# A four-layer diffusion step on one core: products by passes, stores from ScalarE, and a recurrence by eights of chunks

## The chip, the cores and the metric

One core of a Trainium2 chip runs the whole step. The metric is device time in microseconds (us) of one execution, the median of a few runs. Engines by their names in the profile: PE is TensorE (PEld its weight loads), DVE VectorE, ACT ScalarE, POOL GpSimd, SP SyncE, which issues most DMAs.

## The reference

Four layers with different mixers act on 128 context and 512 latent tokens (640 columns in all) of width 1024, inner width E = 2048. Each normalises, projects in, mixes, gates with SiLU(z) and projects out:

```python
for i in range(DEPTH):                        # 0 SSD, 1 gMLP, 2 S5, 3 neighbourhood attention
    hc, gate_c = adaln(xc, norm_g[i], cond_ctx @ w_mod[i] + b_mod[i])
    hl, gate_l = adaln(xl, norm_g[i], cond_lat @ w_mod[i] + b_mod[i])
    yc, yl = mixer[i](hc @ w_in[i]), mixer[i](hl @ w_in[i])
    xc = xc + gate_c * (yc @ w_out[i])
    xl = xl + gate_l * (yl @ w_out[i])
```

The third layer (`kind == 2`) is S5: 128 groups of 16 channels, each with 64 complex states, run over time in both directions, then a GLU:

```python
drv = einsum('gnj,blgj->blgn', bb, seq)       # complex drive
drv[:, 0] += ab * h0
s = associative_scan(complex_combine, (ab, drv))   # s[t] = ab * s[t-1] + drv[t]
y = gelu(y_forward + flip(y_backward) + d_skip * uu)
y = y * sigmoid(y @ w_glu + b_glu)
return y * silu(z), final_state
```

The final S5 state of the context is an output too.

## The kernel before

**Units.** All projections go through `stream` (L249). A unit is one weight tile of 128 x 1024, that is 8 blocks of 128 x 128. For fp32 accuracy it is split into `whi` and `wlo`, and the activations into `hhi` and `hlo`; a unit is 8 steps (slots), and a step is three products, (whi, hhi), (whi, hlo), (wlo, hhi), each two matmuls of 320 columns: 48 matmuls a unit. `unit` (L218) makes the parts: SP loads `raw` (two buffers, L212), ScalarE writes `wlo` = -raw, a POOL DMA adds `raw` to it in flight, and ScalarE casts `whi`. Where `N.adds` is off (from the end of layer 3's input stage on) VectorE or POOL subtracts instead. Unit i is made one unit ahead, with three buffers for each part. Units 0 and 1 of a layer, and the last two ahead of a seam, are walked by halves of the columns (`s` not None); `pairs` names three units whose order is changed.

**Layer 3.** `S5.run` (L1610) builds lists of work by slot and `play` (L330) emits them between the slots of the stream. The queues of TensorE, VectorE, ScalarE and POOL keep that order of emission; SP's is ordered by the framework's own planner. PLAN (L1568) is the order of the 32 units of the input projection, u for channels and z for gates: 256 slots. Of each u unit `driven` (L1703) copies the product out, stores it (`ud`) and loads it back as `ur`, turned by chunks of 8 tokens (80 chunks: 64 latent, 16 context). `load_in`, `turn` and `drive` make the drive of a tile of 8 groups into S, [128, 2 directions, 81, 2, 16]. Four u tiles fill one S. When they are there, `scan` (L1732) runs the recurrence over the chunks: 63 steps on VectorE (`steps`, L1752: per direction one product L1758 and two sums L1761), and 16 steps for the context on POOL (`step`, L1763), between the slots that SCAN5 names. Then four responses, OUTS5 giving the slot of each: `load_out` (BC, PQ, Br and `ur` again), `take` (ScalarE and POOL copy S to `zr`), `gen` (POOL and VectorE make `gx`, L1538 and L1551), `answer` (TensorE, L1813), `kernel` (transposes, three copies to `KK`, eight DMAs to `tr`, L1829), `within` (TensorE `t`, L1838; VectorE `r`, L1839; ScalarE's gelu; store to `yd`).

**Turn.** At slot 256 the GLU begins: its first units need y back from `yd`, by `load_y` (L1848, eight DMAs a tile, into the tiles of `hlo` and, for the second four, `gyl`) and `split_y`. `OUT5` and `IN5` are offsets in slots; BG, BM, BY, BI are buffer counts.

Of the kernel before, what the change touches and what calls it, by code (L numbers as in the profile page):

```python
# [117 lines left out]
class Net:  # L118
# [130 lines left out]
    def stream(self, jobs, pairs=None, after=None, ahead=0, cut=None):  # L249
# [46 lines left out]
        for slot in slots:  # L296
            for i, j, s in slot:
# [9 lines left out]
                k = ui * 8 + j  # L307
# [10 lines left out]
                hh, hl = h(k)  # L318
                for wi, (w, hx) in enumerate(((hi, hh), (hi, hl), (lo, hh))):
                    for v, o, c in cols:  # L320
                        mm(p[:m, o:o + c], w[:, j, :], v(hx), start=(k == 0 and wi == 0), stop=(k == 8 * len(units) - 1 and wi == 2))  # L321
# [1261 lines left out]
BG, BM, BY, BI = 3, 4, 2, 3  # L1583


class S5:
# [23 lines left out]
    def run(self, N, h, own, out):  # L1610
# [92 lines left out]
    def driven(self, N, P, p):  # L1703
# [3 lines left out]
        N.nc.sync.dma_start(self.ud[P["kt"]], u)  # L1707
# [24 lines left out]
    def scan(self, N, q, S):  # L1732

        nc, I = N.nc, N.I
# [4 lines left out]
        fin = self.tile(N, [128, 2, 2, 16], "fin", 2)  # L1739
# [12 lines left out]
        def steps(e, c, end, out, tag):  # L1752

            t = [self.tile(N, [128, 2, 32], f"{tag}{d}", 1) for d in range(2)]
            at = c, end - c + 1
            dst = [out[:, d] if out is not None else S[:, d, (c + 1, end - c)[d]] for d in range(2)]
# [6 lines left out]
        def step(e, c, end, out, tag):  # L1763

            src = skew(F[:, :, c, :], 32 * (end - 2 * c + 1))
            dst = out if out is not None else skew(S[:, :, c + 1], 32 * (end - 2 * c - 1))
            t = self.tile(N, [128, 2, 2, 32], tag, 1)
            e.tensor_tensor(t, src[:, None].to_broadcast([128, 2, 2, 32]), A, op=OP.mult)
            for k in range(2):
                e.tensor_tensor(dst, dst, t[:, k].rearrange("p d (r g) -> p d r g", r=2)[:, :, ::1 - 2 * k], op=OP.add)  # L1770
        for c in range(63):
            steps(v, c, 63, None, "sl")
            if c % 4 == 0:
                i = 64 + c // 4
                step(g, i, 143, fin if i == 79 else None, "sc")
                if i == 79:
                    nc.sync.dma_start(N.O["s5"][:, q], fin.rearrange("p d r g -> p d (r g)"))
            yield

    def load_out(self, N, P):  # L1780
        nc, I, kt = N.nc, N.I, P["kt"]
        P["ur"] = self.load_u(N, kt)
# [5 lines left out]
        nc.sync.dma_start(P["B"], N.s5B[:, kt])  # L1788

# [27 lines left out]
    def kernel(self, N, P):  # L1817
# [8 lines left out]
        nc.scalar.copy(KK[:, 112:128], self.D0[:, P["kt"]])  # L1826
        tr = P["tr"] = self.tile(N, [128, 8, 128], "tr", 2)
        for l in range(8):
            nc.sync.dma_start(tr[l::8], KK[:, 16 * (7 - l):16 * (7 - l) + 128])  # L1829

    def within(self, N, P):
# [10 lines left out]
        nc.sync.dma_start(self.yd[kt // 2][kt % 2], ys.rearrange("p g c -> p (g c)"))  # L1842
# [438 lines left out]
```

## Time and profile before

| | us |
|---|---|
| median of 3 runs | 3023.03 (3021.49 to 3030.51) |
| the profiled execution's own time | 3021.86 |
| its span | 3020.1 |
| TensorE busy | 2750.9 (91%), 18412 matmuls |
| VectorE busy | 2051.4 (68%) |
| ScalarE busy | 1472.4 (49%) |
| POOL busy | 1265.0 (42%) |

Layer 1 runs from about 50 to 610 us of the span, its way out to 743, layer 2 to 1180 and its way out to 1320; layer 3's input projection and recurrence to 1884, its GLU to 2085, its way out to 2240; layer 4 to 2885, then the way out and the final norm. A busy share is a mean over all of these. In a group of instructions the idle time is that of the engine just ahead of them, with what ended it; a wait is put down to the releaser that came last. Matmuls overlap, so a mean duration of one is more than their pitch.

### The profile page before, as it was taken

The numbers are of one execution on the slowest core, as the hardware profiler recorded it, in microseconds if no ns is written. First come the engines' busy times: TensorE is split into PE (matmuls) and PEld (weight loads), VectorE is DVE, ScalarE is ACT, GpSimd is POOL, SyncE is SP. The second block draws the span as 40 slices with busy tenths as digits, with TensorE's granted clock in tenths as the row PEclk, the third lists the DMA queues.
The fourth block names the chain that finished last, engine by engine and source line by source line (L and its number), as shares of the span: only waits on it lengthen the run. The fifth ranks groups of instructions, "written<-read, shape, count | busy, mean of one in ns | idle before, by whom it ended". The sixth has DMA issues, their size and how long they took to land. (4 is left out here: it accounts for less than half of the span.)

```text
span 3020.1 us, 50547 instructions
## 1 busy us (share of the span) xinstructions
PE 2750.9 (91%) x18412; PEld 2643.5 (88%) x18412; DVE 2051.4 (68%) x4948; ACT 1472.4 (49%) x2523; POOL 1265.0 (42%) x1452
## 2 busy tenths in 40 slices
PE   6789999999989898999897886999999999999998
PEld 3778888899889888999797776999989999999998
DVE  5987776676689888736877972225956667666842
ACT  5533444444444445356674653444136666666631
POOL 4466666512476773123443540222443333333232
PEclk9899999999999999999898897999999999999999
DMA  7676677687676667968575569323625444444342
GB/s 253 168 186 165 164 182 182 185 283 216 179 214 189 177 195 223 289 194 219 159 215 161 159 162 185 119 92 132 206 85 146 136 130 137 138 129 134 111 179 87
DMA packets 271735, 517.92 MB, mean 171 GB/s; under 512 B 77888, under 2 KB 146944, under 8 KB 270464
## 3 DMA queue, kind: packets, MB, share of 16 engines
q1 hardware_dynamic: 247424, 427.66, 46.2%
q0 software_dynamic: 24064, 87.04, 14.9%
q8 instruction: 146, 2.39, 0.3%
q14 instruction: 101, 0.83, 0.1%
HBM read 333.83 MB, written 65.70 MB: 132 GB/s over the span
## 5 line engine op out<-in xcount | busy, mean ns | idle before, releaser
L321 PE MATMUL acc<-hhi,whi 128*128 128x320 f32 (+2 forms) x3472 | 861.3, 327 | 24.2 <-ACT hhi L204 8.6
L321 PE MATMUL acc<-hhi,wlo 128*128 128x320 f32 (+2 forms) x3472 | 824.2, 317 | 37.7 <-DMA wlo<-raw 36.4
L321 PE MATMUL acc<-hlo,whi 128*128 128x320 f32 (+2 forms) x3472 | 823.8, 317 | 2.5 <-DVE hlo L573 1.3
L321 PEld LDWEIGHTS acc<-hhi,wlo 128*128 128x128 f32 (+1 forms) x3472 | 600.1, 193 | 46.1 <-DMA wlo<-raw 43.5
L321 PEld LDWEIGHTS acc<-hhi,whi 128*128 128x128 f32 (+1 forms) x3472 | 599.0, 195 | 39.9 <-issue 16.5
L321 PEld LDWEIGHTS acc<-hlo,whi 128*128 128x128 f32 (+1 forms) x3472 | 602.9, 194 | 6.8 <-DVE hlo L573 3.1
L205 POOL TENSOR_TENSOR wlo<-raw,whi 128x1024 fp32r<-128x1024 f32 x95 | 244.8, 2578 | 308.9 <-ACT whi L204 295.8
L226 POOL DMA_DIRECT2D wlo<-raw x164 | 145.9, 895 | 540.4 <-ACT wlo L225 497.8
L227 ACT CAST whi<-raw 128x1024 fp32r<-128x1024 f32 (+1 forms) x164 | 170.4, 1039 | 227.5 <-DMA raw<-in_w_mlp_dram 75.4
L225 ACT ACTIVATE wlo<-raw 128x1024 fp32r<-128x1024 f32 (+1 forms) x164 | 173.0, 1056 | 143.0 <-DMA raw<-in_w_mlp_dram 80.9
L433 DVE SCALAR_TENSOR_TENSOR wacc<-wm,conds,wacc 128x512 f32<-128x512 f32 x280 | 222.6, 849 | 19.5 <-DMA wm<-in_w_mod_dram 19.3
L321 PE MATMUL acc<-y,whi 128*128 128x320 f32 (+2 forms) x1024 | 202.3, 314 | 7.0 <-DVE y L205 4.2
L204 ACT CAST whi<-raw 128x1024 fp32r<-128x1024 f32 x125 | 129.4, 1048 | 107.4 <-PE acc L321 84.2
L321 PEld LDWEIGHTS acc<-y,whi 128*128 128x128 f32 x1024 | 163.7, 190 | 9.8 <-DVE y L205 5.1
L1761 DVE TENSOR_TENSOR S<-S,sl 128x32 f32<-128x32 f32 x1008 | 171.3, 224 | 0.0
L909 DVE SCALAR_TENSOR_TENSOR cacc<-pad,vec,cacc 128x644 f32<-128x644 f32 x128 | 154.6, 1208 | 3.8 <-ACT cacc L907 2.0
L2062 ACT ACTIVATE e<-sb,mx 128x384 f32<-128x384 f32 x128 | 78.9, 617 | 96.8 <-DVE mx L2061 94.9
L321 PE MATMUL acc<-y,wlo 128*128 128x320 f32 (+2 forms) x512 | 123.3, 312 | 2.9 <-DMA wlo<-raw 2.8
L1758 DVE TENSOR_TENSOR sl<-S,A 128x64 f32<-128x64 f32 x504 | 125.9, 290 | 0.0
L2095 DVE TENSOR_TENSOR yn<-yn,av 64x128 f32<-64x128 f32 x320 | 90.8, 284 | 42.9 <-ACT yn L2093 34.5
L1876 DVE TENSOR_TENSOR y<-y,sg 128x640 f32<-128x640 f32 x16 | 14.1, 879 | 150.3 <-ACT sg L1875 150.3
L1016 POOL TENSOR_TENSOR dd<-cmat,dt 128x512 f32<-128x512 f32 x80 | 108.4, 1367 | 11.1 <-DVE dt L820 8.6
(407 smaller groups left out, 5504.7 us busy)
## 6 DMA issues: line engine op xcount, KB each, us to landing
wlo<-raw POOLq DMA_DIRECT2D x163, 512.0 KB, 5.3
wm<-in_w_mod_dram SPq DMA_DIRECT2D x96, 512.0 KB, 5.0
raw<-in_w_out_dram SPq DMA_DIRECT2D x64, 512.0 KB, 4.1
raw<-in_w_nat_dram SPq DMA_DIRECT2D x64, 512.0 KB, 3.6
raw<-in_w_ssd_dram SPq DMA_DIRECT2D x48, 512.0 KB, 3.5
raw<-in_w_mlp_dram SPq DMA_DIRECT2D x48, 512.0 KB, 4.0
fb<-fd SPq DMA_DIRECT2D x40, 512.0 KB, 6.3
s5X<-s5gx SPq DMA_DIRECT2D x32, 512.0 KB, 5.5
```

What stands on the lines that cost most here:

```text
L204: (hi_eng or nc.scalar.copy)(hi, src)
L205: (lo_eng or nc.vector).tensor_tensor(lo, src, f(hi), op=OP.subtract)
L225: self.nc.scalar.activation(lo, raw, AF.Copy, scale=-1.0)
L226: self.nc.gpsimd.dma_start(lo, raw, accum_op=OP.add)
L227: self.nc.scalar.copy(hi, raw)
L321: mm(p[:m, o:o + c], w[:, j, :], v(hx), start=(k == 0 and wi == 0), stop=(k == 8 * len(units) - 1 and wi == 2))
L433: e.scalar_tensor_tensor(acc[:, c], w[:, j], a, acc[:, c], op0=OP.mult, op1=OP.add)
L909: nc.vector.scalar_tensor_tensor(acc, pad[:, j:j + 644], w(j), acc, op0=OP.mult, op1=OP.add)
L1016: nc.gpsimd.tensor_tensor(dg.rearrange("p (h l) -> p h l", h=4), N.ident[:, None, :].to_broadcast([128, 4, 128]), self.dt[:, c, 32 * d + 4 ...
L1758: e.tensor_tensor(t[d], F[:, d, at[d], None, :].to_broadcast([128, 2, 32]), A[:, :, d], op=OP.mult)
L1761: e.tensor_tensor(dst[d], dst[d], t[d][:, k].rearrange("p (r g) -> p r g", r=2)[:, ::1 - 2 * k], op=OP.add)
L2095: nc.vector.tensor_tensor(y[r, o], y[r, o], p[r, w:w + 128], op=OP.add)
```

## The change

Four things change.

1. In `stream`, a unit outside the first two, the seam and `pairs` takes its 24 products by passes: (whi, hhi) for all eight blocks, then (whi, hlo), then (wlo, hhi). Each slot still has three products.
2. The stores of `zd`, `ud` and `yd` in layer 3 are issued by ScalarE instead of SP (16 of each).
3. `ur`'s first load is issued two slots after `driven`, its second load six slots after `o` instead of 15 ahead, and the eight DMAs to `tr` three slots after `kernel` (`unroll`).
4. The recurrence goes by blocks of eight chunks: `local` runs seven steps in all ten blocks of a direction at once, `carry` moves the last state of a block to the next block's last, `spread` gives the other seven or eight of a block what came in. It needs the first eight powers of A, which POOL makes beside (`powers`); the context's blocks are in the same instructions, so POOL's 16 steps go. 22 pieces of work are put in 24 places of SCAN5's windows instead of 64. PLAN, OUTS5, SCAN5 and one offset of OUT5 are other numbers; `gx` has 2 buffers for 3, `KK` and `fin` 1 for 2.

```diff
-                hh, hl = h(k)
-                for wi, (w, hx) in enumerate(((hi, hh), (hi, hl), (lo, hh))):
+                items = [(j, wi) for wi in range(3)]
+                if s is None and i >= 2 and not (pairs is not None and pairs <= i < pairs + 3):
+                    items = [((3 * j + x) % 8, (3 * j + x) // 8) for x in range(3)]
+                for kt, wi in items:
+                    k = ui * 8 + kt
+                    hh, hl = h(k)
+                    w, hx = ((hi, hh), (hi, hl), (lo, hh))[wi]
                     for v, o, c in cols:
...
-PLAN = "uuuuuzuuuzzzuuzuuzzuuuuzzzzz"
-OUTS5 = ((80, 8), (139, 7), (188, 8), (228, 7))
-SCAN5 = ((43, 74), (96, 135), (148, 188), (196, 227))
+PLAN = "uuuuuzuuuzzzuuuuzuuuuzzzzzzz"
+OUTS5 = ((78, 8), (122, 7), (176, 8), (218, 7))
+SCAN5 = ((44, 74), (84, 118), (140, 172), (180, 214))
...
-OUT5 = (-15, 0, -5, 0, 5, 7, 9, 17)
+OUT5 = (-15, 0, -2, 0, 5, 7, 9, 17)
...
-BG, BM, BY, BI = 3, 4, 2, 3
+BG, BM, BY, BI = 2, 4, 2, 3
+SX = 1
...
+            put(e + 2, self.load_first, P)
...
-            for i in range(64):
-                put(a + (b - a) * i // 64, lambda N, g: next(g, None), scan)
+            for i in range(24):
+                put(a + (b - a) * i // 24, lambda N, g: next(g, None), scan)
...
+                put_(o + 6, self.load_again, P)
...
+                put_(o + OUT5[6] + 3, self.unroll, P)
...
-        N.nc.sync.dma_start(self.zd[k], z)
+        N.nc.scalar.dma_start(self.zd[k], z)
...
-        N.nc.sync.dma_start(self.ud[P["kt"]], u)
+        N.nc.scalar.dma_start(self.ud[P["kt"]], u)
...
-        fin = self.tile(N, [128, 2, 2, 16], "fin", 2)
+        fin = self.tile(N, [128, 2, 2, 16], "fin", 1)
+        W = self.tile(N, [128, 2, 8, 2, 32], "W8", 1)
...
+        def powers():
+            Wf = W.rearrange("p d b k (r g) -> p d b k r g", r=2)
+            for k in range(2):
+                N.pcopy(Wf[:, :, 0, k, 0], A[:, k, :, 0:16])
+            yield
+            for b in range(1, 8):
+                for d in range(2):
+                    t = self.tile(N, [128, 2, 32], "sc", 1).rearrange("p k (r g) -> p k r g", r=2)
+                    g.tensor_tensor(t, Wf[:, d, b - 1, None, :, 0].to_broadcast([128, 2, 2, 16]),
+                                    A[:, :, d].rearrange("p k (r g) -> p k r g", r=2), op=OP.mult)
+                    g.tensor_tensor(Wf[:, d, b, :, 0], t[:, 0], t[:, 1, ::-1], op=OP.add)
+                if b % 2:
+                    yield
...
+        def move(d, dst, src, w, m):
+            n, nb = m
+            t = self.tile(N, [128, 640], "sx", SX)[:, 0:n * nb * 64]
+            v.tensor_tensor(t.rearrange("p (a b x) -> p a b x", a=n, x=32),
+                            src.rearrange("p a r g -> p a (r g)")[:, :, None, :].to_broadcast([128, n, 2 * nb, 32]),
+                            w.rearrange("p b k x -> p (b k) x")[:, None].to_broadcast([128, n, 2 * nb, 32]), op=OP.mult)
+            t = t.rearrange("p (a b k r g) -> p a b k r g", b=nb, k=2, r=2, g=16)
+            for k in range(2):
+                x, o = (t[:, :, 0, k], dst[:, :, 0]) if nb == 1 else (t[:, 0, :, k], dst[:, 0])
+                v.tensor_tensor(o, o, x[:, :, ::1 - 2 * k], op=OP.add)
+        def local(b):
             for d in range(2):
+                a = 0, -2
+                move(d, places(d, b + 1, a[d], 10)[:, :, None], places(d, b, a[d], 10), A[:, :, d][:, None], (10, 1))
...
+        todo = [lambda b=b: local(b) for b in range(7)]
+        todo += [lambda: carry(1), last]
+        todo += [lambda a=a: carry(a) for a in range(2, 7)]
+        todo += [lambda: spread(9, -1, 7)] + [lambda a=a: spread(a, a, 7) for a in range(1, 7)] + [lambda: spread(7, 7, 8)]
+        beside = powers()
+        for i, f in enumerate(todo):
+            next(beside, None)
+            f()
...
-        KK = self.tile(N, [128, 240], "KK", 2)
+        KK = self.tile(N, [128, 240], "KK", 1)
...
+    def unroll(self, N, P):
         tr = P["tr"] = self.tile(N, [128, 8, 128], "tr", 2)
         for l in range(8):
-            nc.sync.dma_start(tr[l::8], KK[:, 16 * (7 - l):16 * (7 - l) + 128])
+            N.nc.sync.dma_start(tr[l::8], P["KK"][:, 16 * (7 - l):16 * (7 - l) + 128])
...
-        nc.sync.dma_start(self.yd[kt // 2][kt % 2], ys.rearrange("p g c -> p (g c)"))
+        nc.scalar.dma_start(self.yd[kt // 2][kt % 2], ys.rearrange("p g c -> p (g c)"))
```

## Rows read from the trace of the kernel before

**Rows 1.** Stretches: length, busy time (instructions) of five engines, granted clock, DMA share, GB/s.
```profile
743.00:1180.00 437.00, 397.29 (x2628) 388.05 (x2628) 354.38 (x718) 193.54 (x240) 275.29 (x442) 0.95 0.71 198
...
1387.00:1774.00 387.00, 325.51 (x2276) 318.75 (x2275) 339.43 (x1637) 220.88 (x369) 178.23 (x293) 0.90 0.65 176
1774.00:1884.00 110.00, 81.64 (x487) 75.89 (x486) 39.49 (x51) 55.61 (x83) 25.29 (x24) 0.84 0.89 172
```

**Rows 2.** Waits of the whole span: us in total, times, longest.
```profile
PE acc L321 <- DMA wlo<-raw: 43.2, 25, 6.6
```

**Rows 3.** The same view of 743 to 1180 us.
```profile
PE acc L321 <- DMA wlo<-raw: 24.6, 17, 3.6
...
PE D L1449 <- DVE Bb L1516: 9.6, 5, 4.3
```

**Rows 4.** The chain that ended last: start, us, what.
```profile
1863.85 4.28 DMA gyl<-y5d
...
1883.50 194.36 PE acc L321 x1308
```

**Rows 5.** Groups of instructions on the page: busy, mean ns of one, idle before.
```profile
L226 POOL DMA_DIRECT2D wlo<-raw x164 | 145.9, 895 | 540.4 <-ACT wlo L225 497.8
```

**Rows 6.** DMA issues on the page: count, KB each, median us to landing.
```profile
wlo<-raw POOLq DMA_DIRECT2D x163, 512.0 KB, 5.3
```

**Rows 7.** TensorE in order of time: start, us, what, idle before.
```profile
1197.08 0.90 PE L321 MATMUL acc<-yhi,wlo 128*128 128x320 f32 x2 [3.98 <-DMA wlo<-raw]
```

**Rows 8.** VectorE in order of time, in layer 1 and in a scan.
```profile
319.17 3.80 DVE L909 SCALAR_TENSOR_TENSOR cacc<-pad,vec,cacc 128x644 f32<-128x644 f32 x4
...
1708.81 0.19 DVE L1761 TENSOR_TENSOR S<-S,sl 128x32 f32<-128x32 f32 x1
1708.92 0.35 DVE L1758 TENSOR_TENSOR sl<-S,A 128x64 f32<-128x64 f32 x2
1709.19 0.54 DVE L1761 TENSOR_TENSOR S<-S,sl 128x32 f32<-128x32 f32 x4
1709.64 0.35 DVE L1758 TENSOR_TENSOR sl<-S,A 128x64 f32<-128x64 f32 x2
...
1712.54 0.68 DVE L1538 TENSOR_TENSOR gx<-BC,PQ 128x512 f32<-128x512 f32 x1
```

**Rows 9.** Groups of VectorE and POOL between 1387 and 1774 us.
```profile
L1761 DVE TENSOR_TENSOR S<-S,sl 128x32 f32<-128x32 f32 x1008 | 171.3, 224 | 0.0
L1758 DVE TENSOR_TENSOR sl<-S,A 128x64 f32<-128x64 f32 x504 | 125.9, 290 | 0.0
...
L1839 DVE TENSOR_TENSOR r<-yk,t 128x320 f32<-128x320 f32 x22 | 10.1, 482 | 23.3 <-PE t L1838 23.3
...
L1770 POOL TENSOR_TENSOR S<-S,sc 128x64 f32<-128x64 f32 x120 | 42.6, 355 | 9.4
L1768 POOL TENSOR_TENSOR sc<-S,A 128x128 f32<-128x128 f32 x64 | 37.2, 582 | 11.3 <-ACT mT L1701 2.7 <-DVE S L1749 2.2 <-ACT KK L1826 1.7
```

**Rows 10.** VectorE and POOL in order of time, about 1430 us.
```profile
1429.77 4.21 DVE L1758 TENSOR_TENSOR sl<-S,A 128x64 f32<-128x64 f32 x2
...
1430.40 1.36 POOL L1538 TENSOR_TENSOR gy<-BC,PQ 128x512 f32<-128x512 f32 x1
```

**Rows 11.** Waits between 1325 and 1885 us.
```profile
PE t L1838 <- DMA tr<-KK: 20.2, 5, 7.4
```

**Rows 12.** SP's issues in order of time: start, us, what.
```profile
1468.90 5.97 SPq L1829 DMA_DIRECT2D tr<-KK  x8
...
1827.12 3.92 SPq L1853 DMA_DIRECT2D hlo<-y5d  x8
...
1859.37 18.84 SPq L1853 DMA_DIRECT2D gyl<-y5d  x32
```

**Rows 13.** Waits of SP's queue between 1325 and 1885 us.
```profile
SPq L1784 <- DVE gx L1538: 45.6, 6, 15.0
```

**Rows 14.** The instructions of L1707: duration ns min/median/max, first and last start.
```profile
L1707 SPq DMA_DIRECT2D u5d<-r x16: 319/380/572, 1336.3 to 1663.0; - x16
```

More of the change, by code (lines that the diff above doesn't have):

```diff
@@ L306, in stream @@
                     make(x)
-                k = ui * 8 + j
                 base = A0
@@ L317, in stream @@
                     cols = [(cut.ys[s], a, b - a)]
-                hh, hl = h(k)
-                for wi, (w, hx) in enumerate(((hi, hh), (hi, hl), (lo, hh))):
+                items = [(j, wi) for wi in range(3)]
[5 more added lines that the diff above has]
+                    w, hx = ((hi, hh), (hi, hl), (lo, hh))[wi]
                     for v, o, c in cols:
-                        mm(p[:m, o:o + c], w[:, j, :], v(hx), start=(k == 0 and wi == 0), stop=(k == 8 * len(units) - 1 and wi == 2))
+                        mm(p[:m, o:o + c], w[:, kt, :], v(hx), start=(k == 0 and wi == 0), stop=(k == 8 * len(units) - 1 and wi == 2))
+                k = ui * 8 + j
                 step += 1
@@ L1706, in driven, with load_first @@
         N.nc.scalar.copy(u, p)
-        N.nc.sync.dma_start(self.ud[P["kt"]], u)
+        N.nc.scalar.dma_start(self.ud[P["kt"]], u)
+    def load_first(self, N, P):
         P["ur"] = self.load_u(N, P["kt"])
@@ L1750, in scan @@
         yield
[L1752 to L1756, printed above, removed]
-            for d in range(2):
-                e.tensor_tensor(t[d], F[:, d, at[d], None, :].to_broadcast([128, 2, 32]), A[:, :, d], op=OP.mult)
-            for k in range(2):
-                for d in range(2):
-                    e.tensor_tensor(dst[d], dst[d], t[d][:, k].rearrange("p (r g) -> p r g", r=2)[:, ::1 - 2 * k], op=OP.add)
@@ L1763, in step @@
[L1763 to L1777, printed above, removed]
+        def powers():
[11 more added lines that the diff above has]
+                    yield
+            Wf = W.rearrange("p d b k (r g) -> p (d b) k r g", r=2)
+            N.pcopy(Wf[:, :, 0, 1], Wf[:, :, 0, 0])
+            g.tensor_scalar(Wf[:, :, 1, 1], Wf[:, :, 1, 0], -1.0, 0.0, op0=OP.mult, op1=OP.add)
+            yield
@@ new lines, in places @@
+        def places(d, b, a0, n):
+            if d == 0:
+                return S[:, 0, 8 * a0 + b:8 * (a0 + n - 1) + b + 1:8]
+            return S[:, 1, 64 - 8 * (a0 + n - 1) - b:64 - 8 * a0 - b + 1:8]
+        def move(d, dst, src, w, m):
[8 more added lines that the diff above has]
+                v.tensor_tensor(o, o, x[:, :, ::1 - 2 * k], op=OP.add)
@@ new lines, in local, with carry @@
+        def local(b):
+            for d in range(2):
+                a = 0, -2
+                move(d, places(d, b + 1, a[d], 10)[:, :, None], places(d, b, a[d], 10), A[:, :, d][:, None], (10, 1))
+        def carry(a):
+            for d in range(2):
+                if a > 1:
+                    o, i = places(d, 7, a, 1), places(d, 7, a - 1, 1)
+                elif d == 0:
+                    o, i = S[:, 0, 15:80:64], S[:, 0, 7:72:64]
+                else:
+                    o, i = S[:, 1, 49:66:16], S[:, 1, 57:74:16]
+                move(d, o[:, :, None], i, W[:, d, 7:8], (2 if a == 1 else 1, 1))
@@ new lines, in spread, with last @@
+        def spread(af, ab, nb):
+            for d, a in enumerate((af, ab)):
+                o = S[:, 0, 8 * a:8 * a + 8] if d == 0 else S[:, 1, 57 - 8 * a:65 - 8 * a][:, ::-1]
+                move(d, o[:, None, 0:nb], places(d, 7, a - 1, 1), W[:, d, 0:nb], (1, nb))
+        def last():
+            t = self.tile(N, [128, 640], "sx", SX)[:, 0:128].rearrange("p (k d x) -> p k d x", k=2, d=2)
+            v.tensor_tensor(t, skew(F[:, :, 79, :], 32 * -14)[:, None].to_broadcast([128, 2, 2, 32]), A, op=OP.mult)
+            for k in range(2):
+                v.tensor_tensor(fin, fin, t[:, k].rearrange("p d (r g) -> p d r g", r=2)[:, :, ::1 - 2 * k], op=OP.add)
@@ new lines, in scan @@
+        todo = [lambda b=b: local(b) for b in range(7)]
[6 more added lines that the diff above has]
+            f()
+            if i == 15:
+                nc.sync.dma_start(N.O["s5"][:, q], fin.rearrange("p d r g -> p d (r g)"))
@@ L1781, in load_out @@
         nc, I, kt = N.nc, N.I, P["kt"]
-        P["ur"] = self.load_u(N, kt)
         P["U"] = self.tile(N, [128, 2, 2, 8, 16], "BC", 2)
@@ L1788, in load_out, with load_again @@
         nc.sync.dma_start(P["B"], N.s5B[:, kt])
+    def load_again(self, N, P):
+        P["ur"] = self.load_u(N, P["kt"])
     def take(self, N, P):
@@ L1826 @@
         nc.scalar.copy(KK[:, 112:128], self.D0[:, P["kt"]])
+        P["KK"] = KK
+    def unroll(self, N, P):
         tr = P["tr"] = self.tile(N, [128, 8, 128], "tr", 2)
         for l in range(8):
-            nc.sync.dma_start(tr[l::8], KK[:, 16 * (7 - l):16 * (7 - l) + 128])
+            N.nc.sync.dma_start(tr[l::8], P["KK"][:, 16 * (7 - l):16 * (7 - l) + 128])
     def within(self, N, P):
```

## The prediction

> **What bounds the kernel now.** Read the stretches first [rows 1]. In layer 2 (743 to 1180 us) TensorE is busy 397 of 437 us at a granted clock of 0.95; in layer 3's input stage (1387 to 1774) only 325 of 387 at 0.90, and in its turn to the GLU (1774 to 1884) 82 of 110 at 0.84. In that input stage VectorE has most: 339 of 387. So time can come from TensorE's short waits ahead of layer 3, and from layer 3. The GLU behind it runs one matmul each 0.149 us without a wait (194.36 us for 1308) [rows 4]; nothing is to be had there.
>
> Then the waits. TensorE waits 43.2 us, 25 times, longest 6.6, for `wlo` [rows 2], 24.6 us of it in layer 2 [rows 3]. In layer 3 the chain runs through VectorE's recurrence (L1758, L1761) to 1774, then through SP's small transfers.
>
> **Products by passes.** No matmul, load or byte is added: a unit's 24 products are reordered so that `wlo` is first read by the 17th, 32 matmuls later, 32 x 0.149 = 4.8 us. `wlo` is late rather than `whi` because behind ScalarE's first pass it needs POOL's issue, 0.90 us, and 5.3 us of landing [rows 5, 6]; `whi` needs only ScalarE's second pass. So a wait under 4.8 us ends locally. Some 10 of the 43 us lie where the old order stays (a layer's seam, the units of `pairs`: 3.98 us at 1197 is one [rows 7]) or in layer 3, counted below; 33 can go. What is late next: the raw tiles (two buffers) and, in layer 2, VectorE's tables, for which TensorE already waits 9.6 us in five places [rows 3] and which an earlier TensorE meets sooner. The bounds are 0 (all given back to VectorE) and 33 plus some 5 for a clock that dips less. I take somewhat more than half: **-18 us**.
>
> **The recurrence.** Before, a scan is 63 steps of two products (64 elements a partition) and four sums (32), the two directions alternating. From one step to the next 0.72 us pass [rows 8], 63 x 0.72 = 45.4 us. The rows also show the hop: a sum that needs a product starts 0.27 us after it, while of two independent products the second follows at 0.13 (0.35 for both, 0.22 each). Four dependent 644-element operations take 3.80 us, a pitch near 0.95 [rows 8].
>
> After, 129 instructions: 7 `local` x 2 directions of one product of 640 and two sums of 320; 16 `spread` of 448 (two of them 512) and twice 224; 10 `carry` of 64 and twice 32; two of 128 and twice 64, and `last`. Each needs the one before it, and one buffer (`sx`) serves both directions. Durations lie on a line between 0.19 (32 elements) and 0.68 (512) [rows 8]: 640 gives 0.81, 448 0.61, 320 0.48, 224 0.39, 128 0.29, 64 0.22. With 0.05 us more a hop: 14 x 1.92 = 26.9, 16 x 1.54 = 24.6, 10 x 0.75 = 7.5, 1.8 and 0.9: 61.7 us. If a product need not wait for the sums ahead of it (0.13 less, 43 times) 56; if no hop showed at all (129 x 0.13) 45. I take 58, since the rows show the hop: 12.5 us more a scan, **+50 for four**. There are fewer instructions, but twice the elements.
>
> POOL's part shrinks. Its 64 steps took 37.2 + 42.6 us [rows 9]; the new powers are 32 short instructions a scan, by the same rows some 0.25 to 0.35 us each, 12 us a scan, 48 in all. POOL and VectorE get in each other's way: while POOL made three products of 512 (1.36 us each), one pair of VectorE's took 4.21 us in place of 0.35 [rows 10]. So 32 us less POOL is worth 0 to 32; short operations leave gaps, and I take 0.4 of it: **-13**. The collisions with POOL's response products stay.
>
> **The plan and SP.** VectorE then has 339 + 37 = 376 us of work in a stretch that took 387 with 48 idle. Of that idle time 23.3 us is `r` waiting for TensorE's `t` [rows 9], which itself waits 20.2 us for `tr` [rows 11], whose eight issues cost SP 5.97 us a time [rows 12]; and SP stood 45.6 us, 15.0 at the longest, behind `BC`'s buffer [rows 13], with the raw tiles behind it. The change takes 48 stores off SP at 0.38 us each [rows 14], 18 us, with their waits, issues `ur`'s load later, and leaves fewer empty slots (the four scans fill 130 of 170 slots, before 141 of 184). I take 16 us of idle time to remain: **-32**. The ends are 48 (nothing won) and 5.
>
> What the moves add: ScalarE issues 48 stores. No row shows ScalarE issuing; the nearest is SP's 0.32 to 0.57 us [rows 14], so 0 to 27 us on an engine that is busy 221 of 387; I take nothing on the path, but behind each issue `zr`, `mT` and the next unit's casts queue. `KK` has one buffer for two: the next `KK` copy waits until eight issues (5.97) are through and landed, and all that is behind it on ScalarE waits too. The kernels are 7 or 8 slots of 387/184 = 2.1 us apart, some 15 us, and `unroll` is issued 3 slots later: 0 to 3 us of slack, so 0 to 40 us in 16 times, 0 taken. `gx` with two buffers for three makes POOL wait for TensorE's `answer`, with `wlo`'s issue behind it; the passes are the cover, 4.8 us.
>
> **The turn.** Before, 109 us pass from the last step (1774) to the steady GLU (1883.5), through `tr` and 64 small loads of y; the last 32 alone hold SP 18.84 us [rows 12]. After, the last `within` stands at slot 256 in place of 266, but 42 slots remain behind the scan in place of 29. A slot without waits is 325 x 0.90 / 184 = 1.6 us; 37 slots to 251, where the first y tile is free, 59; then 2, four times 3.92 for the first loads [rows 12], 18.8 for the others, 4.3 of landing [rows 4] and 1.5 for a split (two operations of 640): 101 us. **-8**, between -25 (loads issued ahead) and +5.
>
> **Sum.** Layer 3: 50 - 13 - 32 - 8 = -3, and about -1 for its own `wlo` waits. With the passes' -18: -22 against the profiled execution's 3021.86 us (span 3020.1; the median of the runs is 3023.03): **3000 us**.
>
> **Rivals.** *Slower: the long hop.* The recurrence becomes the stage's clock. If a scan takes 62 us (+65 in all) and 40 us of idle time stay, layer 3 changes by 65 - 13 - 8 - 5 = +39; with -16 by passes about 3045. It decides at 58 us a scan with 35 idle: above both, layer 3 eats the passes. For it: 339 of 387 busy, and the hop. Against: 48 us idle, much of it behind SP.
>
> *Nothing net.* The waits only move: `wlo`'s becomes one for tables or raw tiles, and layer 3 pays for its scan what its plan gains: 3016, from 3012 to 3028.
>
> *Shorter: the cost per instruction decides.* As a mechanism of this kernel: if each VectorE instruction held its engine for its whole duration, a step would cost 2 x 0.22 + 4 x 0.19 = 1.20 us, 76 a scan, and the new one 129 durations, 55 us: 21 less in place of 12 more, 84 in four, of which some 35 reach the end before TensorE and SP take over; with 18 by passes and 18 by plan and turn about 2951. Against it stands the pitch of 0.72; for it, that the scans' groups are busy 171.3 and 125.9 us now, collisions included [rows 9]. [...]
>
> **How the numbers follow.** The forecast (2980 to 3014) 0.45, shorter 0.17, nothing net 0.18, slower 0.20. Half of "shorter" lies below 2950 and half of "slower" above 3042: the range is 2950 to 3042. Measurement of this kernel tells about 0.3%, 9 us, from no change. Faster is 0.42 of the forecast's, 0.17 and 0.02: 0.61; the same 0.19; slower 0.20.
>
> **What would show it.** Passes: TensorE's waits for `wlo` below 12 us, those for VectorE's tables above 10. Recurrence: about 58 us of VectorE a scan without collisions, a pitch near duration plus 0.05; POOL's own part near 12. Plan: `r` waiting for `t` below 15 us, the last scan's end about 1760 (1740 to 1785), the steady GLU some 101 us later. The prediction falls if `KK` copies stand first among ScalarE's waits, if `wlo`'s issue waits on POOL behind `gx`, or if sums follow products without a gap.

## The result, and the profile after

The changed kernel takes 3078.26 us (median of 4, 3073.97 to 3081.86) where the kernel before took 3024.99 beside it: ratio 1.0161, interval 1.0142 to 1.0179, 53 us slower where 22 faster was forecast. Its profiled execution took 3077.96 us (span 3075.9). In the code behind the edits line numbers have moved: L321 is now L326, L1538 and L1551 are L1544 and L1557, L1758 and L1761 are L1797 and L1803, L1829 is L1900, L1839 is L1910, L1853 is L1924.

The same three stretches as in [rows 1]: layer 2, the recurrences (from the first to the end of the last), and the way from there to the GLU.

```profile
743.00:1180.00 437.00, 392.53 (x2597) 384.57 (x2598) 351.37 (x718) 188.43 (x233) 273.56 (x441) 0.95 0.70 195
...
1395.00:1806.00 411.00, 318.38 (x2185) 311.55 (x2183) 339.88 (x640) 217.71 (x363) 168.81 (x217) 0.87 0.57 160
1806.00:1936.00 130.00, 94.53 (x566) 89.40 (x567) 47.70 (x56) 61.71 (x91) 31.95 (x29) 0.80 0.78 173
```

Layer 2 is not shorter: from its first `ln_s` to its last `mixl` it takes 425.0 us for 420.6. The recurrences' stretch takes 411 us for 387, with VectorE busy as long as before (340) and idle 71 for 48; the way to the GLU takes 130 for 110. TensorE waits more in both: its busy share falls from 84 to 77% and from 74 to 73%, and the mean granted clock with it (0.90 to 0.87, 0.84 to 0.80).

TensorE's waits of layer 2 (743 to 1184 us), as [rows 3]:

```profile
PE D L1455 <- DVE Bb L1522: 17.5, 8, 4.5
...
PE acc L326 <- DMA wlo<-raw: 4.8, 4, 2.5
```

The waits for `wlo` went from 24.6 to 4.8 us there; those for VectorE's table rose from 9.6 to 17.5. Over the whole span, as [rows 2], the 43.2 us became:

```profile
PE acc L326 <- DMA wlo<-raw: 7.4, 7, 2.5
```

VectorE in the first recurrence, in order of time, as [rows 8]:

```profile
1397.30 0.82 DVE L1797 TENSOR_TENSOR sx<-S,A 128x640 f32<-128x640 f32 x1
...
1399.21 0.82 DVE L1797 TENSOR_TENSOR sx<-S,A 128x640 f32<-128x640 f32 x1
```

A `local` move repeats after 1.91 us; the sum worked with 1.92. The whole of VectorE's instructions of the four recurrences (`sl` before, `sx` after, with the sums into S; busy time behind the length of the stretch):

```profile
1387.00:1774.00 387.00, 258.64 (x1512) 0.90 0.65 176
...
1395.00:1806.00 411.00, 260.95 (x516) 0.87 0.57 160
```

So before, a scan took VectorE 64.7 us in its place, not the 45.4 of undisturbed steps. Beside POOL's steps for the context a step took 1.11 us (1386.83 to 1387.94) where an undisturbed one takes 0.72 [rows 8]:

```profile
1386.83 0.32 DVE L1758 TENSOR_TENSOR sl<-S,A 128x64 f32<-128x64 f32 x2
...
1387.05 0.53 POOL L1768 TENSOR_TENSOR sc<-S,A 128x128 f32<-128x128 f32 x1 [2.71 <-ACT mT L1701]
...
1387.94 0.51 DVE L1758 TENSOR_TENSOR sl<-S,A 128x64 f32<-128x64 f32 x2
```

The first scan, 45.4 us if nothing disturbed it, ran from 1386.8 to 1446.9: 60.1 us. After the change the first one takes 64.8 (1395.2 to 1460.1).

Groups of VectorE and POOL from 1395 to 1806, as [rows 9]:

```profile
L1803 DVE TENSOR_TENSOR S<-S,sx 128x320 f32<-128x320 f32 (+3 forms) x336 | 146.9, 437 | 11.5
...
L1544 DVE TENSOR_TENSOR gx<-BC,PQ 128x512 f32<-128x512 f32 x36 | 33.3, 952 | 24.0 <-PE y L1881 24.0
...
L1910 DVE TENSOR_TENSOR r<-yk,t 128x320 f32<-128x320 f32 x22 | 10.0, 482 | 19.2 <-PE t L1909 16.5 <-issue 2.6
...
L1776 POOL TENSOR_TENSOR sc<-W,A 128x64 f32<-128x64 f32 x53 | 33.8, 639 | 3.5
L1778 POOL TENSOR_TENSOR W<-sc 128x32 f32<-128x32 f32 x54 | 26.0, 482 | 4.2
```

`r` waits less for `t` (16.5 for 23.3), but `gx` now waits 24.0 us for TensorE. Before, with three buffers, it was 3.1:

```profile
L1538 DVE TENSOR_TENSOR gx<-BC,PQ 128x512 f32<-128x512 f32 x38 | 31.2, 846 | 3.2 <-PE y L1813 3.1
```

Of VectorE's 71 idle us, 54 are such waits (47.5 before); the other 17 are gaps of some 0.03 us ahead of each of the recurrence's 516 instructions (11.5 us ahead of the sums), which the old steps do not have (0.0 in [rows 9]). With these gaps a new scan takes 69.5 us in its place. POOL's powers take 0.64 and 0.48 us an instruction, not the 0.25 to 0.35 assumed.

SP's issues on the way to the GLU, as [rows 12], and the end of the chain:

```profile
1862.44 6.55 SPq L1900 DMA_DIRECT2D tr<-KK  x8
1871.92 2.18 SPq L1900 DMA_DIRECT2D tr<-KK  x3
1874.98 5.62 SPq L1924 DMA_DIRECT2D hlo<-y5d  x8
1880.64 3.10 SPq L1900 DMA_DIRECT2D tr<-KK  x5
1883.85 17.63 SPq L1924 DMA_DIRECT2D hlo<-y5d  x24
1902.01 22.42 SPq L1924 DMA_DIRECT2D gyl<-y5d  x32
```

```profile
1925.23 4.53 DMA raw<-in_w_glu_dram
...
1929.84 1.05 ACT whi L204
...
1932.93 12.21 PE acc L326 x73
```

The first 8 of the 64 loads of y stand among the issues of the last `tr`, the other 56 in one line behind it, and behind them the weight tile of the GLU with which the chain goes on. Before, the first 32 were issued by 1836, beside the last responses.

### The profile page after: what moved, and what is told of

Same layout as the page of the kernel before. It is cut to its first block, busy times and chain, and to the rows that moved or that the text cites. A ratio compares the mean times of both kernels' runs of the same rounds, so it can differ in the third digit from the quotient of the medians.

```text
span 3075.9 us, 49413 instructions
## 1 busy us (share of the span) xinstructions
PE 2757.1 (90%) x18412; PEld 2646.2 (86%) x18412; DVE 2096.3 (68%) x3952; ACT 1478.3 (48%) x2525; POOL 1271.4 (41%) x1388
## 4 chain that ended last, share of the span: by engine, by line
PE 32%; DVE 29%; DMA 10%; POOL 8%; ACT 7%; issue 6%; SPq 1%; ACTq 0%; DVEq 0%; POOLq 0%
PE acc L326 25%; DVE S L1803 4%; DVE sx L1797 3%; DVE wacc L439 3%; DMA wlo<-raw 2%; DVE e L2135 2%; DMA wm<-in_w_mod_dram 2%; POOL dd L1022 2%; DVE cacc L915 2%; POOL dd L1029 1%; ACT e L2133 1%; DVE sb L2130 1%; DVE yn L2166 1%; DVE pt L205 1%; ACT zr L1615 1%
## 5 line engine op out<-in xcount | busy, mean ns | idle before, releaser
L326 PE MATMUL acc<-hhi,whi 128*128 128x320 f32 (+2 forms) x3472 | 630.3, 322 | 26.7 <-DVE x L610 9.8
L326 PE MATMUL acc<-hlo,whi 128*128 128x320 f32 (+2 forms) x3472 | 635.7, 320 | 2.5 <-DVE hlo L579 1.7
L326 PE MATMUL acc<-hhi,wlo 128*128 128x320 f32 (+2 forms) x3472 | 609.2, 316 | 7.2 <-DMA wlo<-raw 7.2
L326 PEld LDWEIGHTS acc<-hhi,whi 128*128 128x128 f32 (+1 forms) x3472 | 547.9, 195 | 37.3 <-issue 14.2
L326 PEld LDWEIGHTS acc<-hlo,whi 128*128 128x128 f32 (+1 forms) x3472 | 547.6, 194 | 9.2 <-DVE hlo L579 4.0
L326 PEld LDWEIGHTS acc<-hhi,wlo 128*128 128x128 f32 (+1 forms) x3472 | 540.1, 192 | 13.8 <-DMA wlo<-raw 9.0
L326 PE MATMUL acc<-y,whi 128*128 128x320 f32 (+2 forms) x1024 | 177.9, 314 | 7.2 <-DVE y L746 3.1
L326 PEld LDWEIGHTS acc<-y,whi 128*128 128x128 f32 x1024 | 157.9, 191 | 10.3 <-DVE y L746 4.5
L2135 DVE TENSOR_SCALAR e<-e,mx 128x384 f32<-128x384 f32 (+1 forms) x160 | 154.3, 964 | 4.2
L1803 DVE TENSOR_TENSOR S<-S,sx 128x320 f32<-128x320 f32 (+3 forms) x336 | 146.9, 437 | 11.5
L1881 PE MATMUL y<-zr,gx 128*128 128x112 f32 x512 | 75.0, 305 | 60.4 <-ACT S L1615 18.5
L1881 PEld LDWEIGHTS y<-zr,gx 128*128 128x128 f32 x512 | 70.6, 217 | 64.5 <-issue 19.5
L1547 POOL TENSOR_TENSOR s5gy<-Bu,Qt 128x512 f32<-128x512 f32 x64 | 88.5, 1415 | 58.9 <-DVE s5gx L1557 58.0
```

Of the source, the lines that this page charges most:

```text
L326: mm(p[:m, o:o + c], w[:, kt, :], v(hx), start=(k == 0 and wi == 0), stop=(k == 8 * len(units) - 1 and wi == 2))
L1803: v.tensor_tensor(o, o, x[:, :, ::1 - 2 * k], op=OP.add)
L1881: nc.tensor.matmul(p[:, 112 * g:112 * g + 112], x[:, d, g], zr[:, d, 4 * s + g], start=(d == 0), stop=(d == 1))
L2135: nc.vector.tensor_scalar(e[:, :w], e[:, :w], m[:, 3:4], None, op0=OP.mult)
```

## The experiments

The ratios go by runs of the kernel before made beside each (their medians lie from 3024.99 to 3029.86). Two lengths are read in each trace: layer 3 from its first copied product (the first `r` of `driven`) to the first `sg` of the GLU, and from the last sum `r` of `within` to that `sg`. They come from rows like these, of the changed kernel (duration ns min/median/max, first and last start):

```profile
L1716 ACT COPY r<-acc x16: 677/696/711, 1340.1 to 1687.4; 128x640 f32<-128x640 f32 x16
...
L1946 ACT ACTIVATE sg<-acc,vec x16: 795/797/797, 1939.5 to 2145.1; 128x640 f32<-128x640 f32 x16
...
L1910 DVE TENSOR_TENSOR r<-yk,t x32: 474/484/489, 1515.8 to 1894.3; 128x320 f32<-128x320 f32 x32
```

| kernel | us, median | ratio to before, interval | layer 3 to the GLU | last r to sg |
|---|---|---|---|---|
| before | 3024.99 | 1 | 551.8 | 29.8 |
| e1 passes alone | 3023.43 | 0.9986 (0.9970 to 1.0003) | 548.4 | 29.8 |
| e10 later loads alone | 3028.18 | 1.0005 (0.9990 to 1.0020) | 551.7 | 30.2 |
| e15 stores alone | 3037.60 | 1.0037 (1.0023 to 1.0051) | 560.8 | 29.5 |
| e18 store of u alone | 3031.21 | 1.0004 (0.9990 to 1.0019) | 557.7 | 30.1 |
| e19 stores of z and y alone | 3031.07 | 1.0015 (1.0003 to 1.0028) | 554.5 | 29.6 |
| e2 stores and later loads | 3038.25 | 1.0030 (1.0013 to 1.0046) | 562.5 | 28.7 |
| e3 recurrence and buffers alone | 3057.70 | 1.0099 (1.0074 to 1.0124) | 576.6 | 34.0 |
| e16 the same, interleaved | 3047.69 | 1.0065 (1.0049 to 1.0082) | 569.3 | 34.4 |
| changed, old recurrence (e5) | 3057.22 | 1.0097 (1.0072 to 1.0122) | 584.1 | 44.2 |
| changed, old recurrence and buffers (e9) | 3054.00 | 1.0091 (1.0066 to 1.0116) | 577.0 | 46.3 |
| changed, old plan (e8) | 3063.16 | 1.0109 (1.0077 to 1.0140) | 588.6 | 34.4 |
| changed, last responses later (e14) | 3072.64 | 1.0144 (1.0129 to 1.0160) | 594.1 | 29.8 |
| changed, stores on SP (e20) | 3077.29 | 1.0163 (1.0141 to 1.0186) | 602.7 | 42.9 |
| changed | 3078.26 | 1.0161 (1.0142 to 1.0179) | 599.4 | 45.2 |
| e12 passes up to the turn | 3015.46 | 0.9961 (0.9946 to 0.9977) | 548.6 | 28.6 |

Where no two lines differ in code, single executions still scatter: the first `r` of the eight profiled kernels without passes, whose code ahead of it is the same, starts from 1335.6 to 1349.2 us (mean 1343.6), and the profile of before is the earliest of them. With passes it is 1329.5 to 1342.5 in eight, mean 1336.3. So the 4.5 us that the changed kernel seems to be late there says nothing; on average the passes gain 7. They do so ahead of layer 2, whose first `ln_s` starts at 755.5 us on average with passes and 763.8 without; layer 2 itself takes 427.1 us with them and 425.0 without.

**Passes alone (e1).**

```diff
+                items = [(j, wi) for wi in range(3)]
+                if s is None and i >= 2 and not (pairs is not None and pairs <= i < pairs + 3):
+                    items = [((3 * j + x) % 8, (3 * j + x) // 8) for x in range(3)]
```

> The kernel before with the products by passes and nothing else. My prediction's term is -18 us (bounds 0 to -38). The trace of the whole change puts the first driven 4.5 us LATER than before although TensorE's waits for wlo shrank from 43 to 7 us. Theory 'waits move' (the time goes to other waits of TensorE, whi and VectorE's tables above all, and layer 4's VectorE work gets slower): 3020 to 3033, no gain. Theory 'passes gain, and something else in the change loses it': 3000 to 3010, and the first driven before 1325 us.

3023.43 us, 4 us faster (9 faster to 1 slower). Layer 3 is 3.4 us shorter and what lies ahead of it some 7, but from the first `sg` to the end it takes 1140.3 us for 1132.7: 7.6 are given back (some 5 by all traces: 1137.3 on average in the seven with passes there, 1132.0 in the nine without). In layer 4 (2240 to 2890 us) VectorE's scaling of `e` is slow:

```profile
L2070 DVE TENSOR_SCALAR e<-e,mx 128x384 f32<-128x384 f32 (+1 forms) x160 | 152.3, 952 | 4.2
```

In order of time, one of them and POOL beside it:

```profile
2500.72 2.57 DVE L2070 TENSOR_SCALAR e<-e,mx 128x384 f32<-128x384 f32 x1
...
2500.67 2.40 POOL L205 TENSOR_TENSOR wlo<-raw,whi 128x1024 fp32r<-128x1024 f32 x1 [0.76 <-ACT e L2068]
```

There `wlo` comes from a subtraction on POOL. With passes this one starts behind ScalarE's `e` and so beside VectorE's, which takes 2.57 us; in the trace of before, with POOL idle, the same scaling takes 0.40 and 0.42 us (at 2502.30 and 2505.33). Of the time that POOL waits ahead of these subtractions in layer 4, `e` ends 60.3 of 113.1 us in the changed kernel; before, `whi` ended 162.1 of 174.8. Without passes the group's mean is 625 ns (before, and e12 below). The first theory, that the waits move, has it in the main; the 7 us ahead of layer 3 are a real gain.

**Passes up to the turn, and a second queue (e12).**

```diff
-                if s is None and i >= 2 and not (pairs
+                if s is None and self.adds and i >= 2 and not (pairs
...
-            N.nc.sync.dma_start(f(lo[16 * i:16 * i + 16])
+            (N.nc.scalar if k >= 4 and i % 2 else N.nc.sync).dma_start(f(lo[16 * i:16 * i + 16])
```

> The kernel before with products by passes only while POOL's transfer makes wlo (up to the turn to the GLU), and with half of the last 32 small loads of y issued by ScalarE beside SyncE. Passes everywhere gained 9 us up to the last sg and gave 7 back in layer 4, where VectorE's e (952 ns in place of 625) runs against POOL's subtraction. Theory 'they collide': the give-back goes, and the turn loses up to 9 of its 18.8 us of loads: 3003 to 3015 where before takes about 3028, ratio about 0.994. Rival 'the gain ahead of layer 3 is a wait that comes back anyway, and the landing, not the issue, ends the turn': 3020 to 3026.

3015.46 us, 0.9961 (0.9946 to 0.9977): 12 us faster, and the best kernel here. The give-back is gone (1131.9 us from `sg` to the end), and so is its cause:

```profile
L2070 DVE TENSOR_SCALAR e<-e,mx 128x384 f32<-128x384 f32 (+1 forms) x160 | 99.9, 625 | 4.3
```

The second queue brought nothing that shows: layer 3 is as long as in e1 (548.6 and 548.4), so the 12 us are those of the passes. SP's issue of all 32 in e1, then the two queues with 16 each in e12:

```profile
1849.81 18.94 SPq L1859 DMA_DIRECT2D gyl<-y5d  x32
```

```profile
1857.85 17.86 SPq L1859 DMA_DIRECT2D gyl<-y5d  x16
...
1856.74 17.09 ACTq L1859 DMA_DIRECT2D gyl<-y5d  x16
```

Half the loads held SP 17.86 us, all of them 18.94. So the number of loads that SP issues is not the price that I read from [rows 12]; what paces them is not shown.

**Queues: stores and later loads (e2), later loads alone (e10), stores alone (e15), and their parts (e18, e19).** The edits are the `scalar.dma_start` lines and `load_first`, `load_again`, `unroll` of the change; e18 moves the store of `ud` only, e19 those of `zd` and `yd`.

> The kernel before with the three kinds of stores issued by ScalarE and the dependent loads later (ur two slots after driven and six after o, the eight DMAs to tr three slots after kernel); scan, plan and buffers as before. Theory 'the scan is the clock': the queues are not the cause, 3010 to 3030. Rival 'ScalarE pays for the stores' (48 issues at up to 0.57 us, with zr, mT and casts behind them): 3035 to 3055.

> The kernel before with only the later loads (ur two slots after driven and six after o, the eight DMAs to tr three slots after kernel); the stores stay on SyncE. Together with ScalarE's stores this cost 10 us, and TensorE waited 38 us for tr where it waited 20. Theory 'tr comes too late': the later loads alone cost it, 3033 to 3045, and the wait for tr stays above 35. Rival 'ScalarE pays for the stores': 3022 to 3030, the wait for tr back near 20.

> The kernel before with only the three stores issued by ScalarE; loads where they were. Later loads alone cost nothing, stores and later loads together 10 us, of which some 7 arise between the second and the third copied unit: there SyncE issued two loads of ix and the responses' tables ahead of the first ur, and TensorE waited for it. Theory 'ScalarE's stores alone do it' (an issue takes 0.33 us of ScalarE's queue, and SyncE's order changes with them): 3035 to 3042. Rival 'only both together do': 3024 to 3032.

> The kernel before with one store of three, that of u (ud), issued by ScalarE; those of z and y stay on SyncE, loads where they were. All three together cost 10 us. Behind ud stands a load of the same data (ur), on SyncE; behind zd and yd stand loads some 100 us later or at the turn. Theory 'SyncE issues the dependent load later once the store is not its own' (the third copied unit 24 us behind the first, where before it was 19): ud alone costs most of it, 3034 to 3042. Rival 'every issue on ScalarE costs its 0.33 us and what stands behind it': a third of the 10, 3028 to 3033, the third unit near 19 to 20.

> The kernel before with the stores of z and y issued by ScalarE and that of u on SyncE. All three cost 10 us, u alone 1 (-3 to +6). Theory 'the stores of z and y cost the rest' (at the turn SyncE's loads of y follow a store that is no longer its own): 3034 to 3040, the third unit at 19 us again, the time from the last r to the first sg or the last units longer. Rival 'they only cost together, SyncE's order being another with all three gone': 3025 to 3032.

The later loads cost nothing, although TensorE's wait for `tr` rises to 37.5 us (20.2 in [rows 11]): that wait costs no time here, against the theory of e10. The stores alone cost some 10 us (7 to 15), as expected. Their issue is cheap, 0.33 us each on ScalarE; but the load that depends on them goes out later. In order of time, e10, where SP issues the store:

```profile
1349.88 0.32 SPq L1710 DMA_DIRECT2D u5d<-r  x1
...
1353.26 0.37 SPq L1684 DMA_DIRECT2D ur<-u5d  x1
```

and e2, where ScalarE does (`ur` 5.4 us behind the store for 3.4):

```profile
1344.67 0.35 ACTq L1710 DMA_DIRECT2D u5d<-r  x1
...
1350.05 0.37 SPq L1684 DMA_DIRECT2D ur<-u5d  x1
...
1357.22 3.67 PE L1730 MATMUL drv<-ur,mT 128*128 128x80 f32 x16 [3.66 <-DMA ur<-u5d]
```

It is not the order of SP's queue alone that does it: this store landed 5.3 us behind its issue (3.3 in e10), and SP stood waiting for that (its waits from 1343 to 1352 us):

```profile
SPq L1684 <- DMA u5d<-r: 3.9, 2, 3.5
```

The third unit is copied 26 us behind the first (e2, e18), 24 (e15), but 19 in before, e10 and e19. So the store of u does this, as expected. In e18's trace layer 3 keeps 5.9 us of these 7 (557.7 for 551.8), while its median is 1 us above before (3 less to 6 more). e19 costs 4.5 us (1 to 8.5), 2.7 by its layer 3. By the medians the two parts are some 6 of the 10, by layer 3 8.6 of 9.0: a cost that arises only with all stores moved is not shown.

**The recurrence alone (e3), and interleaved (e16).** e3 takes `scan` with its 24 places, `gx` in 2 buffers and `KK` in 1 into the kernel before. In e16 the directions alternate:

```diff
-            for d in range(2):
-                move(d, ...)
+            both(*[(d, ...) for d in range(2)])      # two products, then sums of k=0 for both, of k=1 for both
-            t = self.tile(N, [128, 640], "sx", SX)
+            t, at, made = self.tile(N, [128, 896], "sx", SX), 0, []
```

> The kernel before with the new recurrence in its old windows, and the buffers that make room for it (gx 2 for 3, KK 1 for 2); plan and queues as before. Theory 'the scan is the clock': a scan has 61.7 us of dependent VectorE work in place of 45.4, so the last scan ends 30 to 60 us later than 1774 and the time is 3055 to 3080. Rival 'the plan and the turn cost it': 3020 to 3040, since the windows are those of before.

> The kernel before with the new recurrence and its smaller buffers, as in the run that took 3058, but with the two directions interleaved: both products, then the four sums in turn, so that no sum directly follows what it needs. For room the products are kept in 896 elements (local goes by 7 and by 3 blocks: twice the instructions there) and A, h0 and fin share fewer buffers. Theory 'the hop': by the durations in the trace, with 0.09 us less for each instruction that need not wait, a scan takes some 48 us of VectorE in place of 61.7, and of the 30 us that the recurrence cost at least half comes back: 3028 to 3044. Rival 'elements, GpSimd's powers or the smaller buffers cost it, not the hop': a scan still takes 58 or more, the time 3050 to 3060.

In e16 the final state of one direction starts from the state's row instead of the last drive, so that this output differs; the instructions are as many. e3 costs 30 us, e16 20. Two `spread` moves in e3, and in e16 the same two directions:

```profile
1433.57 0.62 DVE L1786 TENSOR_TENSOR sx<-S,W 128x448 f32<-128x448 f32 x1
1434.23 0.82 DVE L1792 TENSOR_TENSOR S<-S,sx 128x224 f32<-128x224 f32 x2
1435.09 0.63 DVE L1786 TENSOR_TENSOR sx<-S,W 128x448 f32<-128x448 f32 x1
...
1436.60 0.63 DVE L1786 TENSOR_TENSOR sx<-S,W 128x448 f32<-128x448 f32 x1
...
1440.28 4.26 DVE L1792 TENSOR_TENSOR S<-S,sx 128x224 f32<-128x224 f32 x2
```

```profile
1431.45 1.16 DVE L1788 TENSOR_TENSOR sx<-S,W 128x448 f32<-128x448 f32 x2
1432.52 1.29 DVE L1795 TENSOR_TENSOR S<-S,sx 128x224 f32<-128x224 f32 x4
1433.85 1.16 DVE L1788 TENSOR_TENSOR sx<-S,W 128x448 f32<-128x448 f32 x2
```

The six instructions repeat after 2.40 us interleaved and 3.03 in a chain (1433.57 to 1436.60): the hop is 0.63 / 6 = 0.10 us an instruction. The first recurrence runs from 1396.64 to 1461.43 in e3, 64.8 us, of which one meeting with POOL's products is 3.4: 61.4. In e16 it is 58.4, less 3.5 for the same: 54.9, not the 48 expected, since the 7 + 3 blocks double `local`'s instructions and ran 3.74 us for 3.83. So a third of the 30 us is the hop's. The other 20 are not VectorE's time in the recurrence: in e16 that is 249 us for the four scans, less than the 259 of before. Its waits are longer (65 us for 47.5), most of all the one of `gx` for TensorE:

```profile
1396.70:1800.00 403.30, 249.36 (x684) 0.89 0.63 169
...
L1538 DVE TENSOR_TENSOR gx<-BC,PQ 128x512 f32<-128x512 f32 x38 | 38.5, 1039 | 23.2 <-PE y L1878 23.2
```

Two buffers of `gx` for three, and pieces of work that are longer and stand between fewer slots, both go with it; these two runs do not part them. In e3 the scans take 272.7 us with their gaps, 14 more than before: the theory's 45.4 us for the old scan holds for undisturbed steps only.

**The change with the old recurrence (e5), and with its buffers too (e9).**

> The changed kernel with the recurrence of before (63 steps on VectorE, 16 on POOL, in 64 places of the new windows); passes, queues, plan and the smaller buffers stay. Theory 'the scan is the clock': the last scan's end comes back from 1806 towards 1775, the time is 3020 to 3045. Rival 'plan, turn and buffers cost it': 3060 to 3080, with the last scan ending near 1800 and the turn still above 125 us.

> The changed kernel with the recurrence of before, and with gx in 3 and KK in 2 buffers again; passes, queues and plan stay. With the smaller buffers it took 3057. Theory 'the smaller buffers cost' (in that run VectorE and POOL waited 58 us for TensorE ahead of gx, none of it before the change): 3035 to 3047, those waits gone. Rival 'plan and turn cost': 3052 to 3060, the waits only move.

With 63 steps again 21 us come back, and 32 us of layer 3's loss stay: both theories had a part. The buffers bring 3 us of the whole (within the noise; 7 in layer 3), the rival's way. These waits are in e5; in e9 VectorE's is 5.1 us and POOL's is gone:

```profile
DVE gx L1544 <- PE y L1827: 37.4, 9, 8.7
...
POOL gx L1544 <- PE y L1827: 20.8, 5, 7.8
```

58 us of waits on two engines, 3 us of time: most of them moved.

**The change with the old plan (e8), with its last responses later (e14), with its stores on SP (e20).**

```diff
-OUTS5 = ((78, 8), (122, 7), (176, 8), (218, 7))
+OUTS5 = ((78, 8), (122, 7), (176, 8), (228, 7))
```

(This is e14; e8 puts PLAN, OUTS5, SCAN5 and OUT5 back, e20 the three `sync.dma_start`.)

> The changed kernel with the numbers of before for PLAN, OUTS5, SCAN5 and OUT5; passes, queues, new recurrence and the smaller buffers stay. So far: passes alone -5, queues alone +10, recurrence with its smaller buffers in the old windows +30, the whole change +53; the change with the old recurrence still +29. Theory 'the plan exposes the turn' (the stream reaches slot 251, and the first loads of y, only behind the last responses; those 64 loads then stand bare on SyncE): the plan costs some 15 to 25 us of the whole, so 3052 to 3064, the time from the last r to the first sg falls from 45 to about 30. Rival 'the parts only add, the plan helps the new recurrence for which it was laid out': 3075 or more.

> The changed kernel with one number changed: the last four responses begin at slot 228 in place of 218, as before the change, so that the input projection (TensorE's slots up to 251, which free the tiles of the first y) ends ahead of the last responses and the first 32 loads of y run beside them. Theory 'the plan exposes the turn': the time from the last r to the first sg falls from 45 to about 30 us and 10 to 16 us come back: 3062 to 3068. Rival 'the responses are the stage's end and simply come 10 slots later': the last r is up to 20 us later and the time 3075 to 3095.

> The changed kernel with its three stores back on SyncE; passes, later loads, recurrence, buffers and plan stay. Theory 'the parts add': 10 us come back, 3064 to 3071. Rival 'in the new plan SyncE is the tighter queue, which the stores relieve there': 3076 or more.

The old plan gives 15 us back. In layer 3 it is 11, all between last `r` and `sg` (45.2 to 34.4): the last `r` comes 554.2 us behind the first copy with either plan. e14, by one number, brings that way to 29.8, as expected, but the last `r` comes 10 us later (564.3 us), so 5.6 of 15 remain (their intervals overlap): theory and rival each to about a half. SP in e14:

```profile
1861.15 17.34 SPq L1924 DMA_DIRECT2D hlo<-y5d  x24
1883.24 6.22 SPq L1900 DMA_DIRECT2D tr<-KK  x8
1890.35 4.26 SPq L1924 DMA_DIRECT2D hlo<-y5d  x8
1894.75 5.24 SPq L1900 DMA_DIRECT2D tr<-KK  x8
```

The first 32 loads are again between the last `tr`. e20 changes nothing, the rival's way: in the full change the stores cost no time that shows, though alone they cost 10. Here the parts do not add.

## Why the prediction was wrong

- **Plan and SP, -32: the step that failed.** I took 48 us of VectorE's idle time for something that an earlier order and a lighter SP could win, leaving 16. Its waits became 54: those of `gx` for TensorE rose by 21 us (3.1 to 24.0), while those for POOL's products fell by 13 and that of `r` for `t` by 7. The buffers of `gx` are not the reason: with three of them and the old recurrence the new plan has 55 us of such waits (e9), and with the old plan the change has 47 (e8). With the old recurrence the change is still 29 us slower, and the plan as such costs 15 (e8; most of it in the turn), where 32 were to be won. VectorE was not idle for lack of earlier slots: work emitted earlier held up the stream instead. With the old recurrence the 17th product is copied 253 us behind the first in e9, in the old plan 228 (e2; the passes do not move it, 216 in e1 for 215), while the last unit of u, which the last recurrence needs and which stands two units earlier in the plan, comes only 3 us earlier (334 and 337).
- **Turn, -8: wrong by some 25.** From the last recurrence to the steady GLU 127 us (1806.2 to 1932.9) pass for the 101 of the sum and the 109 of before. The first load of y went out after 69 us for 59 (a slot 1.9 us for 1.6), the first 32 took 26.5 us (1875.0 to 1901.5) for 17.7, the last 32 22.4 for 18.8, and the weight tile behind them 4.5. By ending the responses with the stream, the plan takes away the work that hid 32 loads; I had the loads bare in the sum, but priced by rows in which they ran beside responses. With the last responses later, from the last `r` to `sg` is again as short as before (e14).
- **Recurrence, +50, and POOL's steps less, -13: together +37 in the sum, +19 in the trace.** The four scans with their gaps took 258.6 us of VectorE before and 278 after. The working of the new scan was right: with every hop it was 61.7 us, I took 58, and the first one of e3 has 61.4 without its meeting. The old scan was the slip: 45.4 us is 63 undisturbed steps, but it took 64.7 in its place, and the 171.3 and 125.9 us of [rows 9] (74 a scan, overlaps counted twice) pointed at it. What VectorE loses against undisturbed rows went from 77 us (4 x 19.3) to 32 (4 x 8.1): 45 less, an estimate, where 13 were taken. POOL's own time fell less than assumed: 59.8 us of the powers' two groups and 9 of their copies, for the 79.8 of [rows 9]. By the table the recurrence costs +30 in the old windows with its buffers and +21 in the new plan. So this term was nearer than its parts, by two errors against each other. Fewer instructions did not make the scan shorter: undisturbed 45.4 us for 378 instructions, 61.4 for 129; in place 64.7 and 69.5.
- **Passes, -18: mechanism right, size wrong, and one step missing.** `wlo`'s waits fell as told (43.2 to 7.4, below 12) and VectorE's table waits rose above 10. In layer 2, where 24.6 us stood, nothing came of it: the bound "all given back". 7 us reach layer 3, and the passes also ran where POOL subtracts, which I did not cost: 5 to 8 back in layer 4, which e12 shows by leaving them out there. Without that they are worth 12. The 5 us for the clock were an estimate: the mean granted clock of whole runs is 0.958 with the passes alone (e1) and 0.954 in the runs of before beside them; in layer 2 it is 0.95 in the traces of before and after. The cover is 4.2 us, not 4.8: `wlo`'s first reader moves from the third product to the 17th, 28 matmuls of 0.149 us [rows 4], an estimate.
- **Stores, KK, gx at 0.** Stores alone cost 10, within the 27 stated, but not in the full change; `KK` did not become ScalarE's first wait; `gx`'s wait appears (24 us of VectorE) and is worth 3 of the whole or 7 in layer 3 by e5 and e9.
- **The rival "long hop" came nearest** (3045): hop and idle time were beyond its point of 58 with 35, as it asks. It still fell 33 short: it kept -8 for the turn, where +17 stand, and -16 for the passes; and its +65 for the scans is more than the trace has, so part of its nearness is luck.

By stretches of the two traces, 19 us of the recurrences' stretch were lost against the sum (24 longer where 5 were expected: 19 by the scans, 6.5 by waits, 2 less by other work) and 25 in the turn; the rest is ahead of layer 3, where the single traces scatter, and in layer 4.

## What to carry over

Idle time of an engine that is emitted in a fixed order was no reserve here (VectorE's waits went from 47.5 to 54 us): before counting on it, ask which in-order stream would have to wait instead. When stages overlap, price what follows the last step by what it will then stand beside: where the last responses ended with the stream, from the last `r` to `sg` took 45.2 us, and where they hid 32 of the loads of y 29.8 (before, and e14). Price old and new work beside the same neighbours: the old steps took 0.72 us alone and 1.1 beside POOL's, so taking those away was worth more than I gave for it. And count elements besides instructions: undisturbed, the recurrence with a third of the instructions and twice the elements took a third longer (61.4 us for 45.4).

## What the runs showed of the hardware that was not expected

- Two queues did not issue 32 small loads faster than one: 18.94 us for 32 on SP (e1), 17.86 and 17.09 for 16 each on SP and ScalarE at the same time (e12).
- A VectorE scaling of 128x384 took 2.57 us beside a POOL subtraction of 2.40 us (e1), and 0.40 and 0.42 with POOL idle (before); the 160 of its group average 952 ns in e1 and 625 in before and e12.
- 63 steps of 64- and 32-element VectorE instructions come to 45.4 us at their undisturbed pitch of 0.72 and took 60.1 in the first scan, where POOL ran its own short steps beside them and three products of 512.
- Issued by ScalarE, the first store of u landed 5.3 us behind its issue (e2), by SP 3.3 (e10).
- Back to back, six VectorE instructions of 448 and 224 elements took 3.03 us where each needs the one before (e3), and 2.40 where none does (e16).
